# i and f rows inside the stick-breaking heads, two gates moved to the last head, transposes at the loop's front and values at its end

## The chip, the cores and the metric

The kernel runs on one core of one Trainium2 chip. The metric is the device time of one execution in microseconds (us). The profiled execution is taken apart below: PE is the matrix engine (TensorE), DVE the vector engine, ACT the scalar engine, POOL GpSimd, and SP the queue that issues most transfers. Each engine works through its own instructions in the order in which they were written to it; that order is fixed when the kernel is built.

## The reference, cut to what matters

One block of a hybrid encoder, 512 tokens of width 1024: stick-breaking attention (8 heads of 128), an mLSTM (4 heads of 256) and cross-attention (4 heads) read one normalised input; each branch is projected, gated and summed, then comes an MLP. The change concerns the first two branches, the gates and the first projections.

```python
def _stick_breaking(q, k, v):
    ...
        z = jnp.einsum('bhqd,bhkd->bhqk', qb, kf[:, :, :end]) * scale
        log_1m = jnp.where(causal, jax.nn.log_sigmoid(-z), 0.0)
        later = lax.cumsum(log_1m, axis=3, reverse=True) - log_1m
        log_a = jnp.where(causal, jax.nn.log_sigmoid(z) + later, -jnp.inf)
        outs.append(jnp.einsum('bhqk,bhkd->bhqd', jnp.exp(log_a), vf[:, :, :end]))
...
def _mlstm(q, k, v, i_pre, f_pre):
    log_f = jax.nn.log_sigmoid(f_pre.astype(f32))
    ...
        bcum = jnp.cumsum(lfc, axis=-1)
        d = jnp.where(tri, bcum[..., :, None] - bcum[..., None, :] + ic[..., None, :], -jnp.inf)
        m_t = jnp.maximum(m_inter, jnp.max(d, axis=-1))
...
        i_pre = (ml_i + b_if[l, :ML_HEADS]).transpose(0, 2, 1)
        f_pre = (ml_f + b_if[l, ML_HEADS:]).transpose(0, 2, 1)
...
        gates = jax.nn.sigmoid(gate_pre + b_gate[l]).reshape(bsz, seq, N_BRANCH, D_MODEL)
        mixed = (gates[:, :, 0] * (y_sb @ w_sb_proj[l])
                 + gates[:, :, 1] * (y_ml @ w_ml_proj[l])
                 + gates[:, :, 2] * (y_x @ w_x_proj[l]))
        x = x + mixed @ w_out[l]
```

## The kernel before, in words

Everything is kept in 128-partition tiles. A matrix product in near-f32 precision is made of three matmuls in a reduced format (`mm3`, L86 to L88): high by high, high by low, low by high. So a weight tile of 128x1024 (`load_w`, L80) is loaded by SP into one of 3 `raw` buffers, rounded by ACT into `whi` (L76), and its rest put by DVE into `wlo` (L77), 4 buffers of each. `projT` then runs 24 matmuls of 512 columns on it into one of two PSUM banks called `pj`. The banks called `tr` are two as well, those called `q4` four.

The stages in the order of time are the memory's keys and values, the products with V, O and gate weights, cross-attention, stick-breaking (about 350 to 512 us of the profile), then the projection of the stick-breaking result (`proj(0, ...)`), the mLSTM (to about 760 us), `proj(1, ...)`, the output product and the MLP.

The stick-breaking stage is a loop over 8 heads. Its parts are:

- `sb_qk(head)`: two `projT` (48 matmuls, in rows `pj<-h`) and the splits of q and k, for a head two ahead.
- `sb_weights(head)`: the scores z (10 matmuls into four `q4` banks, in rows `q<-k,q`), then per bank on DVE a mask (L764), on ACT Abs, Exp, Ln (L770 to L772), on DVE a minimum (L774) and a scan (L776), on ACT an Exp (L778) that gives A. The bank of 128 columns comes last.
- `sb_transposed(head)`: ten transposes of A (L789) into three `tr` tiles, for j=0 (4), j=1 (3) and j=2, 3 (3). The first transpose needs all four A tiles. As there are two `tr` banks, the third tile waits until the first has been split into `aT` by ACT and DVE (L93, L94).
- `sb_values(head)`: 10 matmuls (rows `tr<-aT,v`) into a `tr` bank, copied by ACT into `yf` (L812).
- `x_proj(n)`: n tiles of the cross-attention's projection (24 matmuls each, rows `pj<-y`); DVE multiplies each by its gate (L604, `mix<-pj,gate`).
- `y_pair`, `gate`: the split of a result into the input of `proj`; a sigmoid of 4 ACT and one DVE instruction (L130 to L134). `gate(0, ...)` and `gate(2, ...)` read finished sums from memory (`gd`), `gate(1, ...)` first runs a `projT`.

In the kernel before, the loop issues q and k, the x_proj tiles, the values of the head before, the scores of the next head, and the transposes of this head; the values of head 7 follow after the loop. Then come the i and f rows of the mLSTM: 16 matmuls (`tr<-h,wif`, L865, L866), a chain of ACT and DVE instructions on 4 partitions (L868 to L883) with two scans, the store of the result to memory, from where it is read back spread over all partitions, and 8 transposes of 4 columns (L898, L899) into the columns `acol` and `em`. Only the mLSTM needs them. In its heads 0, 1 and 2 stand the plain gates 0 to 2, 3 and 4.

A scheduler reorders what the code issues within each engine, by its own costs, so that the written order is a wish; the rows of the order below are what each engine gets.

Of the kernel before, what the change touches and what calls it, by code (L numbers as in the profile page):

```python
# [8 lines left out]
F32 = mybir.dt.float32  # L9
# [6 lines left out]
P = 128  # L16
# [19 lines left out]
def tile_block(ctx: ExitStack, tc: tile.TileContext, xT, x_, memT, mem_, small,  # L36
# [701 lines left out]
    def sb_qk(head):  # L738
        qp = tp.tile([P, 2, T], F32R, tag="qk", bufs=4, name="q")
        kp = tp.tile([P, 2, T], F32R, tag="qk", bufs=4, name="k")  # L740
        for isk, (t, scale) in enumerate(((qp, P ** -0.5), (kp, None))):
            if head < 2:
                o = raws[head, isk]
            else:
                o = pj()
                projT(h, load_w(w_sbqk[isk * NK + head]), o)
            split2(t, o, scale)
        q0 = tp.tile([P, P], F32, tag="q0", bufs=2, name="q0")
        k0 = tp.tile([P, P], F32, tag="k0", bufs=2, name="k0")
        whole(q0, qp[:, :, :P])  # L750
        whole(k0, kp[:, :, :P])
        qks[head] = qp, kp, q0, k0
# [71 lines left out]
    def y_pair(k):  # L824
        t = ytile()
        split2(t, y[k])
        return t

    x_proj.f = 0
    sb_qk(0)  # L830
    sb_weights(0)
    sb_v(0)
    sb_qk(1)
    aT = None
    for head in range(NK):
        if head < NK - 2:
            sb_qk(head + 2)
        x_proj((0, 1, 1, 1, 1, 2, 2, 0)[head])
        if head > 0:
            sb_values(head - 1, aT)  # L840
        if head == NK - 1:
            ys = [y_pair(k) for k in range(NK - 1)]
            gs = [gate(0, f) for f in range(3)]
        if head < NK - 1:
            if head % 2 == 0 and head < NK - 2:
                sb_v(head // 2 + 1)
            sb_weights(head + 1)
        aT = sb_transposed(head)
    sb_values(NK - 1, aT)
    y = ys + [y_pair(NK - 1)]  # L850
    ph.close()


    ph = ExitStack()
    tp = ph.enter_context(tc.tile_pool(name="mlp", bufs=1))


    raw = wp.tile([P, W], F32, tag="raw", bufs=3, name="raw")[:, :NK * NG].rearrange("p (k c) -> p k c", k=NK)
    wif = wp.tile([P, W], F32R, tag="whi", bufs=4, name="wif")[:, :NK * NG].rearrange("p (k c) -> p k c", k=NK)
    nc.sync.dma_start(out=raw, in_=w_if)  # L860
    act.activation(out=wif, in_=raw, func=AF.Copy)
    dve.tensor_tensor(out=wif[:, :, 64:], in0=raw[:, :, 64:], in1=f32(wif[:, :, 64:]), op=ALU.subtract)
    o = tr()
    for k in range(NK):
        pe.matmul(o[:NG, :], wif[:, k], h[k][:, 0, :], start=k == 0, stop=False)  # L865
        pe.matmul(o[:NG, :], wif[:, k], h[k][:, 1, :], start=False, stop=k == NK - 1)  # L866
    ip, fp, fa, mf, fc = (tmp(n)[:4, :] for n in ("ip", "fp", "fa", "mf", "fc"))
    act.activation(out=ip, in_=o[64:68, :], func=AF.Identity, bias=sm[0:4, C_BIF:C_BIF + 1])  # L868
    act.activation(out=fp, in_=o[96:100, :], func=AF.Identity, bias=sm[32:36, C_BIF:C_BIF + 1])
    dve.tensor_tensor(out=ip, in0=o[0:4, :], in1=ip, op=ALU.add)  # L870
    dve.tensor_tensor(out=fp, in0=o[32:36, :], in1=fp, op=ALU.add)
    act.activation(out=fa, in_=fp, func=AF.Abs)
    dve.tensor_scalar(out=mf, in0=fp, scalar1=0.0, scalar2=None, op0=ALU.min)
    act.activation(out=fa, in_=fa, func=AF.Exp, scale=-1.0)
    act.activation(out=fa, in_=fa, func=AF.Ln, bias=1.0)

    dve.tensor_tensor_scan(out=fc, data0=mf, data1=fa, initial=0.0, op0=ALU.add, op1=ALU.subtract)
    dve.tensor_tensor(out=ip, in0=ip, in1=fc, op=ALU.subtract)
    mr = tmp("mr")[:4, :]
    dve.tensor_tensor_scan(out=mr, data0=ip, data1=ip, initial=0.0, op0=ALU.max, op1=ALU.max)  # L880
    dve.tensor_tensor(out=fc, in0=fc, in1=mr, op=ALU.add)
    nm_ = tp.tile([4, T], F32, tag="nm", name="nm")
    dve.tensor_scalar(out=nm_, in0=mr, scalar1=-1.0, scalar2=None, op0=ALU.mult)  # L883

    nmd = dp.tile([4, T], F32, tag="nmd", name="nmd")
    nc.sync.dma_start(out=nmd, in_=nm_)

    def bcast(head):

        t = tp.tile([P, T], F32, tag="b1", bufs=2, name="b1")  # L890
# [2 lines left out]

    b1s = [bcast(0), bcast(1)]
    proj(0, y, gs)
    col = tr()
    for i in range(NT):
        pe.transpose(col[:, 4 * i:4 * i + 4], ip[:, i * P:(i + 1) * P], ident[:4, :4])  # L898
        pe.transpose(col[:, 16 + 4 * i:20 + 4 * i], fc[:, i * P:(i + 1) * P], ident[:4, :4])  # L899
    dve.tensor_copy(out=acol, in_=col[:, :16])  # L900
    act.activation(out=em, in_=col[:, 16:32], func=AF.Exp, scale=-1.0)
    y = [None] * NK
    vs, sos, qks = {}, {}, {}

# [48 lines left out]
    ml_qk(0)  # L953
    ml_v(0)
    ml_o(0)
    gs = []
    for head in range(4):
        q, k = qks[head][:2], qks[head][2:]

        sts, scs, b1 = [], [], b1s[head]  # L960
        bm = tmp("bm")
        dve.tensor_tensor(out=bm.rearrange("p (j c) -> p j c", j=NT), in0=b1.rearrange("p (j c) -> p j c", j=NT),
                          in1=m4.unsqueeze(1).to_broadcast([P, NT, P]), op=ALU.add)
        for j in range(NT):
            c0, c = j * P, slice(j * P, (j + 1) * P)
            st = q4()
            for f in range(2):
                if j < NT - 1:
                    mm3(st[:, c0:], k[f][0][:, 0, c], k[f][0][:, 1, c], q[f][0][:, 0, c0:], q[f][0][:, 1, c0:],
                        f == 0, f == 1)  # L970
                else:
                    pe.matmul(st[:, c0:], k[f][1], q[f][1], start=f == 0, stop=f == 1)
            sts.append(st)
        if head > 0:
            ml_y(head - 1, yts)
        for j in range(NT):
            c0 = j * P
            w = tmp("w")
            ab = acol[:, 4 * j + head:4 * j + head + 1]
            act.activation(out=w[:, c0:c0 + P], in_=bm[:, c0:c0 + P], func=AF.Exp, bias=ab)  # L980
            if j < NT - 1:
                act.activation(out=w[:, c0 + P:], in_=b1[:, c0 + P:], func=AF.Exp, bias=ab)
            dve.scalar_tensor_tensor(out=w[:, c0:], in0=sts[j][:, c0:], scalar=HD ** -0.5, in1=w[:, c0:],
                                     op0=ALU.mult, op1=ALU.mult)
            sc = tp.tile([P, 2, T - c0], F32R, tag=f"sc{j}", name="sc")
            split2(sc, w[:, c0:])
            scs.append(sc)
        if head < 2:
            b1s.append(bcast(head + 2))
        if head < 3:  # L990
            ml_qk(head + 1)
        else:
            gs += [gate(1, 5), gate(1, 6)]
        v, so = vs[head], sos[head]
        nms = []
        dn = tp.tile([P, NT], F32, tag="dn", bufs=2, name="dn")
        ss = tp.tile([P, NT], F32, tag="ssh", bufs=2, name="ssh")
        for i in range(NT):
            nm = q4()
            nms.append(nm)  # L1000
            for j in range(i + 1):
                c = slice((i - j) * P, (i - j + 1) * P)
                mm3(nm[:, :HD + 2], scs[j][:, 0, c], scs[j][:, 1, c], v[j][:, 0, :], v[j][:, 1, :], j == 0, j == i)
            d1 = dn[:, i:i + 1]
            dve.tensor_scalar(out=d1, in0=nm[:, HD:HD + 1], scalar1=-1.0, scalar2=None, op0=ALU.mult)
            dve.scalar_tensor_tensor(out=d1, in0=nm[:, HD:HD + 1], scalar=em[:, 4 * i + head:4 * i + head + 1],
                                     in1=d1, op0=ALU.max, op1=ALU.max)
            dve.reciprocal(out=d1, in_=d1)
            junk = tmp("junk")
            act.activation(out=junk[:, :HD], in_=nm[:, :HD], func=AF.Square, scale=d1, accum_out=ss[:, i:i + 1])  # L1010
        rr = rsqrt_cols(tp, ss, NT, 1.0 / HD, "rh")
        dve.tensor_tensor(out=dn, in0=rr, in1=dn, op=ALU.mult)
        yts = [tmp("yt") for _ in range(2)]
        for i in range(NT):
            c = slice((i % 2) * HD, (i % 2 + 1) * HD)
            dve.scalar_tensor_tensor(out=yts[i // 2][:, c], in0=nms[i][:, :HD], scalar=dn[:, i:i + 1],
                                     in1=so[:, i], op0=ALU.mult, op1=ALU.mult)
        if head < 3:
            gs += [gate(1, f, tr() if f == 2 else None) for f in ((0, 1, 2), (3,), (4,))[head]]
            ml_o(head + 1)  # L1020
            ml_v(head + 1)
        else:
            gs.append(gate(1, 7))
        if head == 3:
            ml_y(head, yts)
# [472 lines left out]
```

## Time and profile before

| | before |
|---|---|
| median of 3 runs | 1135.73 us (1135.08 to 1137.24) |
| the profiled execution | 1135.93 us, of which span 1134.2 us |
| PE busy | 1110.0 us, 98% of the span |
| DVE, ACT, POOL busy | 862.8, 727.6, 129.3 us |
| mean granted TensorE clock | 0.994 |

The span is the time from the first to the last instruction; 1.7 us of the profiled time lie outside it. Busy time of PE counts matmuls as they overlap, so what is left are the moments in which no matmul is under way. "Idle before" in a row is time in which the engine had nothing to do, and the name behind the arrow is what it then waited for last.

### The profile page before, as it was taken

The numbers are of one execution on the slowest core, as the hardware profiler recorded it, in microseconds if no ns is written. First come the engines' busy times: TensorE is split into PE (matmuls) and PEld (weight loads), VectorE is DVE, ScalarE is ACT, GpSimd is POOL, SyncE is SP. The second block draws the span as 40 slices with busy tenths as digits, with TensorE's granted clock in tenths as the row PEclk, the third lists the DMA queues.
The fourth block names the chain that finished last, engine by engine and source line by source line (L and its number), as shares of the span: only waits on it lengthen the run. The fifth ranks groups of instructions, "written<-read, shape, count | busy, mean of one in ns | idle before, by whom it ended". The sixth has DMA issues, their size and how long they took to land.

```text
span 1134.2 us, 16470 instructions
## 1 busy us (share of the span) xinstructions
PE 1110.0 (98%) x6080; PEld 957.8 (84%) x6080; DVE 862.8 (76%) x1267; ACT 727.6 (64%) x1208; POOL 129.3 (11%) x229
## 2 busy tenths in 40 slices
PE   9999999999999999986999999999999999999998
PEld 6778889999987888865888888888888898998997
DVE  5889777778767766666578798768867679688698
ACT  6756654648657867785477787735766466475573
POOL 0112211321101100000000000001011101111110
PEclk9999999999999999997999999999999999999999
DMA  9978888874512332225432322467377878878774
GB/s 358 352 193 236 249 231 273 227 233 143 183 40 96 117 105 96 84 65 177 140 101 88 103 89 75 158 167 157 113 206 169 209 181 204 202 205 212 172 192 112
DMA packets 62680, 190.31 MB, mean 168 GB/s; under 512 B 6788, under 2 KB 13572, under 8 KB 62600
## 3 DMA queue, kind: packets, MB, share of 16 engines
q1 hardware_dynamic: 45880, 131.25, 34.1%
q0 software_dynamic: 16288, 57.68, 24.6%
q8 instruction: 48, 0.79, 0.3%
q10 hardware_dynamic: 432, 0.33, 0.1%
q14 instruction: 32, 0.26, 0.1%
HBM read 172.45 MB, written 16.79 MB: 167 GB/s over the span
## 4 chain that ended last, share of the span: by engine, by line
PE 82%; DVE 8%; ACT 6%; issue 2%; DMA 1%; ACTq 0%; DVEq 0%; POOL 0%; POOLq 0%
PE pj L87 8%; PE pj L86 8%; PE pj L88 8%; PE q L170 5%; PE q L168 5%; PE q L169 5%; PE q L195 4%; PE q L196 4%; PE q L197 4%; PE q L86 3%; PE q L87 3%; PE q L88 3%; PE pj L168 2%; PE pj L169 2%; PE pj L170 2%; PE pj L196 2%
## 5 line engine op out<-in xcount | busy, mean ns | idle before, releaser
L76 ACT ACTIVATE whi<-rq 128x1024 fp32r<-128x1024 f32 x112 | 118.1, 1057 | 111.2 <-PE q L170 26.7
L77 DVE TENSOR_TENSOR wlo<-rq,whi 128x1024 fp32r<-128x1024 f32 x112 | 136.5, 1221 | 57.5 <-ACT whi L76 57.5
L76 ACT ACTIVATE whi<-B 128x1024 fp32r<-128x1024 f32 x84 | 88.5, 1058 | 77.1 <-PE q L196 16.5
L77 DVE TENSOR_TENSOR wlo<-B,whi 128x1024 fp32r<-128x1024 f32 x84 | 102.5, 1222 | 43.4 <-ACT whi L76 43.2
L86 PE MATMUL pj<-h,whi 128*128 128x512 f32 x296 | 116.9, 395 | 0.3 <-ACT mqk L93 0.3
L87 PE MATMUL pj<-h,whi 128*128 128x512 f32 x296 | 116.1, 392 | 0.0
L88 PE MATMUL pj<-h,wlo 128*128 128x512 f32 x296 | 115.9, 391 | 0.0
L76 ACT ACTIVATE whi<-raw 128x1024 fp32r<-128x1024 f32 x72 | 76.0, 1057 | 60.5 <-PE pj L87 47.5
L77 DVE TENSOR_TENSOR wlo<-raw,whi 128x1024 fp32r<-128x1024 f32 x72 | 87.8, 1221 | 31.5 <-ACT whi L76 31.4
L170 PE MATMUL q<-whi,slo 128*128 128x512 f32 (+1 forms) x236 | 91.1, 386 | 0.3 <-DVE slo L94 0.3
L169 PE MATMUL q<-wlo,shi 128*128 128x512 f32 (+1 forms) x236 | 91.1, 386 | 0.1
L168 PE MATMUL q<-whi,shi 128*128 128x512 f32 (+1 forms) x236 | 91.0, 386 | 0.0
L86 PE MATMUL pj<-y,whi 128*128 128x512 f32 x192 | 75.8, 396 | 1.9 <-DVE gt L607 1.9
L87 PE MATMUL pj<-y,whi 128*128 128x512 f32 x192 | 75.5, 393 | 0.0
L88 PE MATMUL pj<-y,wlo 128*128 128x512 f32 x192 | 75.3, 392 | 0.0
L202 POOL DMA_DIRECT2D rq<-in_w_ff_dram x50 | 42.9, 892 | 283.0 <-DVE wlo L77 173.9
L86 PEld LDWEIGHTS pj<-h,whi 128*128 128x128 f32 x296 | 55.6, 188 | 11.8 <-ACT mqk L93 0.7
L88 PEld LDWEIGHTS pj<-h,wlo 128*128 128x128 f32 x296 | 55.6, 188 | 11.3
L87 PEld LDWEIGHTS pj<-h,whi 128*128 128x128 f32 x296 | 55.6, 188 | 10.6
L170 PEld LDWEIGHTS q<-whi,slo 128*128 128x128 f32 x236 | 44.3, 188 | 9.6 <-DVE slo L94 0.7
L169 PEld LDWEIGHTS q<-wlo,shi 128*128 128x128 f32 x236 | 44.3, 188 | 9.3 <-DVE wlo L77 0.5
L168 PEld LDWEIGHTS q<-whi,shi 128*128 128x128 f32 x236 | 44.3, 188 | 8.9
(440 smaller groups left out, 3234.0 us busy)
## 6 DMA issues: line engine op xcount, KB each, us to landing
rq<-in_w_ff_dram SPq DMA_DIRECT2D x56, 512.0 KB, 4.7
rq<-in_w_ff_dram POOLq DMA_DIRECT2D x50, 512.0 KB, 5.7
B<-in_w_vo_dram SPq DMA_DIRECT2D x48, 512.0 KB, 5.5
B<-in_w_vo_dram POOLq DMA_DIRECT2D x24, 512.0 KB, 7.2
raw<-in_w_proj_dram SPq DMA_DIRECT2D x24, 512.0 KB, 3.6
raw<-in_w_sbqk_dram SPq DMA_DIRECT2D x16, 512.0 KB, 3.6
raw<-in_w_mlqk_dram SPq DMA_DIRECT2D x16, 512.0 KB, 3.6
rawk<-in_w_kv_dram SPq DMA_DIRECT2D x14, 512.0 KB, 8.5
```

What stands on the lines that cost most here:

```text
L76: act.activation(out=hi[:, c], in_=raw[:, c], func=AF.Copy)
L77: dve.tensor_tensor(out=lo[:, c], in0=raw[:, c], in1=f32(hi[:, c]), op=ALU.subtract)
L86: pe.matmul(out, lh, rh, start=start, stop=False)
L87: pe.matmul(out, lh, rl, start=False, stop=False)
L88: pe.matmul(out, ll, rh, start=False, stop=stop)
L168: pe.matmul(banks[j][:, c], lh, w[0][:, cw], start=st, stop=False, **mm)
L169: pe.matmul(banks[j][:, c], lh, w[1][:, cw], start=False, stop=False, **mm)
L170: pe.matmul(banks[j][:, c], ll, w[0][:, cw], start=False, stop=sp_, **mm)
L195: pe.matmul(o, wh, uh, start=start and k == 0 and f % 2 == 0, stop=False, **mm)
L196: pe.matmul(o, wh, ul, start=False, stop=False, **mm)
L197: pe.matmul(o, wl, uh, start=False, stop=stop and k == 3, **mm)
L202: pool.dma_start(out=raws[v], in_=w[fh, 2 * kh + v], accum_op=ALU.add)
```

## The change

The i and f rows become a function, `if_rows`, issued in turn 2 of the stick-breaking loop, and the small transposes another, `if_columns`, issued in turn 4. The tiles of the chain are reused in place. In the loop, the transposes of a head are issued first, then q and k, V, the scores of the next head, the x_proj tiles, and the head's own values last. In the last turn two plain gates, `gate(1, 0)` and `gate(1, 1)`, are issued; in the mLSTM head 0 keeps gate 2 alone. No instruction of PE is added or removed.

```diff
+    def if_rows():
+        ...
+        nc.sync.dma_start(out=raw, in_=w_if)
+        ...
+        for k in range(NK):
+            pe.matmul(o[:NG, :], wif[:, k], h[k][:, 0, :], start=k == 0, stop=False)
+            pe.matmul(o[:NG, :], wif[:, k], h[k][:, 1, :], start=False, stop=k == NK - 1)
+        ...
+        dve.tensor_tensor_scan(out=fp, data0=fp, data1=fa, initial=0.0, op0=ALU.add, op1=ALU.subtract)
+        dve.tensor_tensor(out=ip, in0=ip, in1=fp, op=ALU.subtract)
+        dve.tensor_tensor_scan(out=fa, data0=ip, data1=ip, initial=0.0, op0=ALU.max, op1=ALU.max)
+        ...
+        nc.sync.dma_start(out=nmd, in_=fa)
+        return ip, fp
+
+    def if_columns(ip, fc):
+        col = tr()
+        for i in range(NT):
+            pe.transpose(col[:, 4 * i:4 * i + 4], ip[:, i * P:(i + 1) * P], ident[:4, :4])
+            pe.transpose(col[:, 16 + 4 * i:20 + 4 * i], fc[:, i * P:(i + 1) * P], ident[:4, :4])
+        dve.tensor_copy(out=acol, in_=col[:, :16])
+        act.activation(out=em, in_=col[:, 16:32], func=AF.Exp, scale=-1.0)
...
-    aT = None
     for head in range(NK):
+        aT = sb_transposed(head)
         if head < NK - 2:
             sb_qk(head + 2)
+        if head < NK - 1:
+            if head % 2 == 1:
+                sb_v(head // 2 + 1)
+            sb_weights(head + 1)
+        if head == 2:
+            rows_if = if_rows()
+        if head == 4:
+            if_columns(*rows_if)
         x_proj((0, 1, 1, 1, 1, 2, 2, 0)[head])
-        if head > 0:
-            sb_values(head - 1, aT)
         if head == NK - 1:
             ys = [y_pair(k) for k in range(NK - 1)]
+            g1 = [gate(1, f) for f in range(2)]
             gs = [gate(0, f) for f in range(3)]
-        if head < NK - 1:
-            if head % 2 == 0 and head < NK - 2:
-                sb_v(head // 2 + 1)
-            sb_weights(head + 1)
-        aT = sb_transposed(head)
-    sb_values(NK - 1, aT)
+        sb_values(head, aT)
...
-    gs = []
+    gs = g1
     for head in range(4):
...
-            gs += [gate(1, f, tr() if f == 2 else None) for f in ((0, 1, 2), (3,), (4,))[head]]
+            gs += [gate(1, f, tr() if f == 2 else None) for f in ((2,), (3,), (4,))[head]]
```

What stands where on the engines, first on PE in a middle turn of the loop, before: the scores of head 6, the first seven transposes of head 5 right behind them, and projections.

```order
L86 MATMUL q_4660<-k,q 128x512
L87 MATMUL q_4660<-k,q 128x512
L88 MATMUL q_4660<-k,q 128x512
L761 MATMUL q_4674<-k_4358,q_4357 128x128
L789 MATMUL tr<-ident,A 128x128 x7
L86 MATMUL pj<-h,whi 128x512
L87 MATMUL pj<-h,whi 128x512
L88 MATMUL pj<-h,wlo 128x512
```

The same place of the change: the last matmul of a head's values, nine projections, and the first seven transposes of the next head.

```order
L809 MATMUL tr<-aT,v_4428 128x128
L86 MATMUL pj<-h,whi 128x512
L87 MATMUL pj<-h,whi 128x512
L88 MATMUL pj<-h,wlo 128x512
L86 MATMUL pj<-h,whi 128x512
L87 MATMUL pj<-h,whi 128x512
L88 MATMUL pj<-h,wlo 128x512
L86 MATMUL pj<-h,whi 128x512
L87 MATMUL pj<-h,whi 128x512
L88 MATMUL pj<-h,wlo 128x512
L789 MATMUL tr<-ident,A 128x128 x7
L86 MATMUL pj<-h,whi 128x512
```

The transposes of a head moved from one whole turn behind that head's scores to a place behind one x_proj tile (24 matmuls), the values and up to ten projections. In turn 2 the first four stand right behind the values of head 1, with no projection between.

Second, on PE behind the last head, before: the end of the i and f matmuls, six matmuls of `proj(0)` and the first small transpose.

```order
L866 MATMUL tr<-h,wif 100x512
L86 MATMUL pj<-y,whi 128x512
L87 MATMUL pj<-y,whi 128x512
L88 MATMUL pj<-y,wlo 128x512
L86 MATMUL pj<-y,whi 128x512
L87 MATMUL pj<-y,whi 128x512
L88 MATMUL pj<-y,wlo 128x512
L898 MATMUL tr<-ident,ip 128x4
L86 MATMUL pj<-y,whi 128x512
```

In the change the small transposes stand behind the scores of head 5, about one turn and a half behind the i and f matmuls.

```order
L761 MATMUL q_4684<-k_4422,q_4421 128x128
L865 MATMUL tr<-ident,ip 128x4
L866 MATMUL tr<-ident,fp 128x4
L865 MATMUL tr<-ident,ip 128x4
L866 MATMUL tr<-ident,fp 128x4
L865 MATMUL tr<-ident,ip 128x4
L866 MATMUL tr<-ident,fp 128x4
L865 MATMUL tr<-ident,ip 128x4
L866 MATMUL tr<-ident,fp 128x4
L86 MATMUL pj<-y,whi 128x512
```

So between the i and f matmuls and their small transposes there were six matmuls, and now there are a whole turn's.

Third, on ACT at the last head, before: the gates' sigmoids (L130 to L134) stand between the splits of head 7's transposed weights, `aT_5183` to `aT_5200`.

```order
L131 ACTIVATE gate_5172<-gate_5172 128x512
L93 ACTIVATE aT_5183<-tr_5178 128x512
L134 ACTIVATE gate_5164<-gate_5164,sm_70 128x512
L132 ACTIVATE gate_5172<-gate_5172 128x512
L93 ACTIVATE aT_5190<-tr_5186 128x384
L93 ACTIVATE aT_5197<-tr_5193 128x256
L134 ACTIVATE gate_5172<-gate_5172,sm_70 128x512
L794 ACTIVATE aT_5200<-tr_5193 128x128
L812 ACTIVATE yf_5213<-tr_5202 128x512
L93 ACTIVATE y_5215<-yf_5213 128x512
```

In the change they stand between those splits, which come first, and the copy `yf_5338` of head 7's values with its split `y_5340`. The gate 5297 is the plain gate 1.

```order
L132 ACTIVATE gate_5297<-gate_5297 128x512
L132 ACTIVATE gate_5305<-gate_5305 128x512
L130 ACTIVATE gate_5313<-gd_5311,sm_70 128x512
L134 ACTIVATE gate_5297<-gate_5297,sm_70 128x512
L134 ACTIVATE gate_5305<-gate_5305,sm_70 128x512
L131 ACTIVATE gate_5313<-gate_5313 128x512
L130 ACTIVATE gate_5321<-gd_5319,sm_70 128x512
L132 ACTIVATE gate_5313<-gate_5313 128x512
L131 ACTIVATE gate_5321<-gate_5321 128x512
L812 ACTIVATE yf_5338<-tr_5327 128x512
L134 ACTIVATE gate_5313<-gate_5313,sm_70 128x512
L93 ACTIVATE y_5340<-yf_5338 128x512
```

On PE the two plain gates (48 matmuls) now stand between the last transposes of head 7 and its values; behind the values, `proj(0)` runs the seven other heads' parts of its tile 0 and six of tile 1 (39 matmuls) before it reads head 7.

## Rows read from the trace of the kernel before

**Rows 1.** The page's part 1: span, busy time and instructions of each engine.

```profile
span 1134.2 us, 16470 instructions
PE 1110.0 (98%) x6080; PEld 957.8 (84%) x6080; DVE 862.8 (76%) x1267; ACT 727.6 (64%) x1208; POOL 129.3 (11%) x229
```

**Rows 2.** Waits of PE, whole span: total us, times, longest.

```profile
PE tr L898 <- DVE ip L878: 7.4, 1, 7.4
PE tr L789 <- DVE aT L94: 5.4, 7, 2.8
...
PE q L86 <- DVE A L776: 0.7, 1, 0.7
...
PE q L86 <- DVE yt L1016: 0.5, 2, 0.2
```

**Rows 3.** Windows: us, busy (x) of PE, PEld, DVE, ACT, POOL, clock, DMA, GB/s.

```profile
354.00:504.80 150.80, 147.37 (x721) 122.41 (x719) 105.69 (x180) 115.64 (x251) 10.00 (x36) 1.00 0.31 99
504.80:531.20 26.40, 13.31 (x48) 10.03 (x47) 16.49 (x25) 15.04 (x27) 1.05 (x8) 0.74 0.44 140
```

**Rows 4.** PE in order of time behind the last head: start, us, what, idle before.

```profile
507.77 0.52 PE L789 MATMUL tr<-ident,A 128*128 128x128 f32 x3 [2.80 <-DVE aT L94]
509.34 0.50 PE L86 MATMUL tr<-aT,v 128*128 128x512 f32 x1 [1.05 <-DVE aT L94]
...
527.52 0.80 PE L86 MATMUL pj<-y,whi 128*128 128x512 f32 x1 [1.86 <-DVE gt L607]
```

**Rows 5.** Windows of PE alone: us, busy (x), granted clock, DMA share, GB/s.

```profile
510.14:513.96 3.82, 3.82 (x15) 0.55 0.12 30
527.52:531.20 3.68, 3.68 (x10) 0.56 0.41 117
```

**Rows 6.** PE in order of time, inside the loop.

```profile
465.15 0.39 PE L86 MATMUL pj<-y,whi 128*128 128x512 f32 x1
...
470.59 0.39 PE L86 MATMUL tr<-aT,v 128*128 128x512 f32 x1
...
472.31 0.36 PE L86 MATMUL q<-k,q 128*128 128x256 f32 x1
...
488.55 0.36 PE L86 MATMUL q<-k,q 128*128 128x256 f32 x1
...
490.42 0.93 PE L789 MATMUL tr<-ident,A 128*128 128x128 f32 x7
```

**Rows 7.** Waits of PE from 354 to 504.8 us, the loop without its end.

```profile
PE tr L789 <- DVE aT L94: 2.6, 6, 0.5
```

**Rows 8.** DVE in order of time, inside the loop.

```profile
465.35 0.69 DVE L604 TENSOR_TENSOR mix<-pj,gate 128x512 f32<-128x512 f32 x1 [2.75 <-PE pj L88]
...
486.88 1.23 DVE L77 TENSOR_TENSOR wlo<-raw,whi 128x1024 fp32r<-128x1024 f32 x1
...
495.32 1.22 DVE L776 TENSOR_TENSOR_SCAN A<-q,a 128x511 f32<-128x511 f32 x1
496.46 0.26 DVE L774 SCALAR_TENSOR_TENSOR a<-q,a 128x127 f32<-128x127 f32 x1
...
497.24 0.41 DVE L776 TENSOR_TENSOR_SCAN A<-q,a 128x127 f32<-128x127 f32 x1
```

**Rows 9.** ACT in order of time, inside the loop and at its end.

```profile
480.91 0.29 ACT L778 ACTIVATE A<-A 128x128 f32<-128x128 f32 x1
...
497.68 0.31 ACT L778 ACTIVATE A<-A 128x128 f32<-128x128 f32 x1 [0.41 <-DVE A L776]
...
506.80 0.72 ACT L134 ACTIVATE gate<-gate,sm 128x512 f32<-128x512 f32 x1
507.41 0.63 ACT L132 ACTIVATE gate<-gate 128x512 f32<-128x512 f32 x1
...
512.26 0.60 ACT L812 ACTIVATE yf<-tr 128x512 f32<-128x512 f32 x1 [2.33 <-PE tr L809]
512.89 0.63 ACT L93 ACTIVATE y<-yf 128x512 fp32r<-128x512 f32 x1
```

More of the change, by code (lines that the diff above doesn't have):

```diff
@@ L827, in y_pair @@
         return t
+    nmd = dp.tile([4, T], F32, tag="nmd", name="nmd")
+    def if_rows():
+        raw = wp.tile([P, W], F32, tag="raw", bufs=3, name="raw")[:, :NK * NG].rearrange("p (k c) -> p k c", k=NK)
+        wif = wp.tile([P, W], F32R, tag="whi", bufs=4, name="wif")[:, :NK * NG].rearrange("p (k c) -> p k c", k=NK)
+        nc.sync.dma_start(out=raw, in_=w_if)
+        act.activation(out=wif, in_=raw, func=AF.Copy)
+        dve.tensor_tensor(out=wif[:, :, 64:], in0=raw[:, :, 64:], in1=f32(wif[:, :, 64:]), op=ALU.subtract)
+        o = tr()
+        for k in range(NK):
+            pe.matmul(o[:NG, :], wif[:, k], h[k][:, 0, :], start=k == 0, stop=False)
+            pe.matmul(o[:NG, :], wif[:, k], h[k][:, 1, :], start=False, stop=k == NK - 1)
+        ip, fp = (tp.tile([4, T], F32, tag=n, name=n) for n in ("ip", "fp"))
+        fa = tmp("fa")[:4, :]
+        act.activation(out=ip, in_=o[64:68, :], func=AF.Identity, bias=sm[0:4, C_BIF:C_BIF + 1])
+        act.activation(out=fp, in_=o[96:100, :], func=AF.Identity, bias=sm[32:36, C_BIF:C_BIF + 1])
+        dve.tensor_tensor(out=ip, in0=o[0:4, :], in1=ip, op=ALU.add)
+        dve.tensor_tensor(out=fp, in0=o[32:36, :], in1=fp, op=ALU.add)
+        act.activation(out=fa, in_=fp, func=AF.Abs)
+        dve.tensor_scalar(out=fp, in0=fp, scalar1=0.0, scalar2=None, op0=ALU.min)
+        act.activation(out=fa, in_=fa, func=AF.Exp, scale=-1.0)
+        act.activation(out=fa, in_=fa, func=AF.Ln, bias=1.0)
+        dve.tensor_tensor_scan(out=fp, data0=fp, data1=fa, initial=0.0, op0=ALU.add, op1=ALU.subtract)
+        dve.tensor_tensor(out=ip, in0=ip, in1=fp, op=ALU.subtract)
+        dve.tensor_tensor_scan(out=fa, data0=ip, data1=ip, initial=0.0, op0=ALU.max, op1=ALU.max)
+        dve.tensor_tensor(out=fp, in0=fp, in1=fa, op=ALU.add)
+        dve.tensor_scalar(out=fa, in0=fa, scalar1=-1.0, scalar2=None, op0=ALU.mult)
+        nc.sync.dma_start(out=nmd, in_=fa)
[7 more added lines that the diff above has]
+        act.activation(out=em, in_=col[:, 16:32], func=AF.Exp, scale=-1.0)
     x_proj.f = 0
@@ L855, in tile_block @@
     tp = ph.enter_context(tc.tile_pool(name="mlp", bufs=1))
[L858 to L886, printed above, removed]
     def bcast(head):
@@ L895, in tile_block @@
     proj(0, y, gs)
[L896 to L901, printed above, removed]
     y = [None] * NK
```

## The prediction, made before the change was run

> **What bounds the kernel now.** I read the page's first part first: PE is busy for 1110.0 of 1134.2 us [rows 1]. The change moves PE instructions and adds none, so it can win only from the 24.2 us in which PE has nothing under way, and from stretches in which its clock is low. The list of PE's waits says where those lie: one wait of 7.4 us of the first small transpose for the i and f chain (L898 on DVE's `ip`), and seven waits of the third transpose group (L789) of 5.4 us in all, of which one is 2.8 [rows 2]. Then the windows: from 354 to 504.8 us, the loop over the heads without its end, PE is busy for 147.4 of 150.8 us at clock 1.00; the next 26.4 us, to 531.2, hold only 13.3 us of PE work, at clock 0.74 [rows 3]. So one place holds more than half of what PE lacks. In order of time it reads so: the last three transposes of head 7 wait 2.80 us, its values 1.05, the small transpose 7.4, the next matmul of `proj(0)` 1.86 [rows 2, 4]. The order of ACT shows what stands behind the first two: the splits that free the `tr` bank stand behind three gates' sigmoids. The third waits for the whole chain from the i and f matmuls through ACT and DVE, with weight splits queued between on DVE; the fourth for a DVE instruction that stood behind the same chain.
>
> **What is removed.** The four waits: 2.80 + 1.05 + 7.4 + 1.86 = 13.1 us. Where they go: the chain now has a whole turn of the loop, over 70 matmuls, where it had six; the splits of head 7 stand ahead of the gates; and 48 matmuls of the plain gates lie between its transposes and its values. 24 matmuls of 512 columns take from 465.15 to 470.59, 5.44 us, or 0.227 each [rows 6], so the gates give 10.9 us of cover at the place where 3.85 were lost.
>
> **The clock.** Two stretches behind the waits ran at a granted clock of 0.55 and 0.56, near the lower of the two levels (1.2 of 2.4 GHz), for 3.82 and 3.68 us [rows 5]. Elsewhere in the loop it is 1.00 [rows 3]. If the waits go, so does this. By the clock alone it is worth 3.82 x 0.45 + 3.68 x 0.44 = 3.3 us; by the count of the second stretch, ten matmuls that would take 2.27 us at 0.227, it is 1.4 there against 1.6 by the clock. I take 3.0, bounds 2.8 and 3.3.
>
> **What the loop pays: the front transposes.** Before, a head's transposes came a turn after its scores and never waited for A. Now they come behind one x_proj tile, the values (470.59 to 472.31, 1.72 us) and 0 to 10 projections. Two chains decide. (a) From the first score matmul to the last A: 472.31 to 481.20, 8.9 us [rows 6, 9], which had a few splits and one gate step between. The cover from the same point is the scores themselves (488.55 to 490.42, 1.87), x_proj 5.44 and the values 1.72, together 9.0 without a projection, 11.3 with ten. (b) In heads 4 and 5 the DVE order puts x_proj's product with the gate (L604) ahead of the last scans. From the end of the x_proj tile on: start of L604 0.20 later (465.15 to 465.35), L604 0.69, the scan of 511 columns 1.22, 0.26, a weight split 1.23, the scan of 127 columns 0.41 and the Exp 0.31 [rows 6, 8, 9], 4.3 us; neighbours on one engine overlap by about 0.1, so 3.9 to 4.3. The cover is 1.72 plus nine or ten projections, 3.8 to 4.0. So the front transposes wait between 0 and 0.5 us a head. Head 3 has the 16 i and f matmuls as further cover, heads 6 and 7 have two x_proj tiles; that leaves heads 1, 2, 4 and 5, and head 0, whose values come right behind its transposes. Five times 0.3 is 1.5; bounds 0 and 5 (five times 1.0, if a transfer or a split is late as well). The six waits of the third group, 2.6 us [rows 7], have the same cause as before, one bank too few, and I leave them as they are; that they all go is the lower bound. The wait of 0.7 for a scan's bank at the loop's start [rows 2] isn't touched.
>
> **The i and f work inside the loop.** Its instructions on ACT and DVE are the same ones, queued in turn 2. Two of them stand on ACT ahead of head 3's last two Exps, which have the 16 i and f matmuls (3.6 us at 0.227) as cover that no other head has; the rest stand behind head 3's scans and ahead of the splits of its transposes, which are wanted only 19 projections later (4.3 us). I cost it at nothing, since ACT and DVE were busy for 116 and 106 of 150.8 us in the loop [rows 3]; without that slack it would be a wait of the length of the longest third-group wait inside the loop, 0.5 [rows 7]. The weight load of 400 KB and the small store move up in SP's queue, each with one `raw` buffer's turn ahead of it, and nobody waits for the store before the mLSTM.
>
> **The loop's end.** Head 7's values end the gates. ACT then has 13 gate steps before the copy `yf`, at 0.61 from start to start (506.80 to 507.41) 7.9 us, then 0.60, two more steps and the split, 0.63 [rows 9]: some 10.4 us from the end of the gates' matmuls. PE has the values, 1.72, and 39 matmuls that don't need it, 8.9 [rows 6]: 10.6. The gate tile that frees a `pj` bank for the third tile of `proj(0)` comes at about the same time. I take 0.3 us of wait, bounds 0 and 2 (as much as the present 1.86).
>
> **The mLSTM** loses 48 matmuls of cover behind its head 0; the order fills the place with projections of the next head. Heads with one gate behind them wait 0.2 us each now [rows 2]. I take 0.5 in all, bounds 0 and 2.
>
> **The sum.** 13.1 + 3.0 - 1.5 - 0.3 - 0.5 = 13.8 us off the profiled execution's 1135.93, of which 1134.2 is the span; that execution is 0.2 above the median of the runs. So 1122.1, said as **1122.0**.
>
> **A rule against it.** Before, single waits of up to 0.7 us inside the loop left the clock at 1.00 [rows 2, 3]; it fell only behind the long waits at the end [rows 4, 5]. The Trainium skill (TensorE: Matmul & The Clock Gate, section "A second HAM failure mode: psum-queue depth-cycling") says that short idles of PE between groups of matmuls, repeated each turn, can make the clock swing between its two levels, with a loss at each fall. By that rule the front waits that this change spreads over the loop would cost more than their own length; the trace so far disagrees with it.
>
> **The rivals.**
> 1. *The short front waits drop the clock.* Each of five would cost what a fall costs now, about 1.5 us [rows 5]: 7.5 more, 1129.5. Against it: clock 1.00 over the whole loop with seven waits in it. Chance 0.05. This is the mechanism of the rule above.
> 2. *The waits move into the loop, and the kernel is slower.* It needs the projections between values and transposes to be missing or late, so that the chains are met bare: 4.3 - 1.72 = 2.6 us in each of five heads, 13, and a fall of the clock behind each as behind the 2.80 of now, 7.5: 20.5 against 16.1, so 1140. It decides from 3.2 us a head on, clock included. Against it: the order has nine or ten projections there in two of the heads, and DVE and ACT have slack. Chance 0.03; a milder form, 2.5 to 3.2 a head, would end as no change, chance 0.04.
> 3. *Half of it:* front waits, head 7's split and the mLSTM reach their upper bounds (5 + 2 + 2), 1129, or some of them do, from 1125 on. Chance 0.15.
> 4. *Better than said:* the loop's waits vanish with the new order, 2.6 + 2.3 more, about 1117.2. Chance 0.10.
>
> **How the numbers follow.** The forecast's own case, 1119 to 1125, has 0.63. The range for 8 in 10 takes rival 4 in from 1117.5 and the larger part of rival 3, to 1128.0. A measurement of this kernel can tell about 0.2% (2.3 us) from no change. Faster by more: the forecast and rivals 1, 3 and 4, 0.93; within: 0.04; slower: 0.03.
>
> **What would show it.** In the changed profile the waits of the small transposes and of L607 should be gone from PE's list, and the window from the last head into `proj(0)` should be at clock 1.00. The loop should show a few waits of L789 for ACT's A (L778 or its line then) below 0.5 each. Wrong would be: a wait above 2 us anywhere in the loop, a granted clock below 0.95 in a window of the loop, or a wait of `proj(0)` for head 7's split. If PE's idle time fell by 13 us and the time didn't follow, the clock would have taken it.

## The result, and the profile after

The changed kernel takes 1123.09 us (median of 4 runs, 1122.05 to 1124.76) beside 1136.44 for the one before (4 runs, 1135.08 to 1137.24): a ratio of 0.9885, with a 95% interval from 0.9867 to 0.9903. The profiled execution took 1122.05 us, of which the span is 1120.3. Forecast were 1122.0 and 1120.4. The total was right; two of its terms were mis-sized in opposite directions, and what was said of why the waits go turned out to be wrong in part. Of the runs of the kernel before that are compared below, one took 3918.4 us and is left out of the ratios. The page's part 1 of the changed kernel, which answers to [rows 1]:

```profile
span 1120.3 us, 16473 instructions
...
PE 1106.8 (99%) x6080; PEld 954.9 (85%) x6080; DVE 859.7 (77%) x1267; ACT 728.2 (65%) x1208; POOL 126.6 (11%) x229
```

The waits of PE over the whole span, in the columns of [rows 2]:

```profile
PE q L86 <- ACT whi L76: 2.1, 2, 1.2
PE tr L789 <- ACT yf L812: 1.8, 3, 0.9
PE q L86 <- DVE yt L1021: 1.5, 2, 0.9
...
PE tr L789 <- DVE aT L94: 0.7, 1, 0.7
PE pj L86 <- DVE u L937: 0.6, 1, 0.6
PE tr L789 <- ACT A L778: 0.3, 1, 0.3
```

The 7.4, the 1.9 and the 2.8 are gone, and so is the values' 1.05. The loop's waits are about as long as before (2.6 and 2.8), but of another cause: three now wait for the copy `yf` of a head's values (L812), since values and transposes, which share the two `tr` banks, now stand close together; a single one, 0.3, waits for A. One more, 0.7 for the splits `aT`, is that of head 3. The mLSTM's waits (`yt`, `u`) have grown from 0.8 (with one for `mqk`, 0.3) to 2.1. The first row lies in the first 10 us, where these waits differ from run to run.

The windows that answer to [rows 3], in its columns: the loop as before, and behind it a stretch without a gap, at clock 1.00 where it was 0.74.

```profile
354.00:504.80 150.80, 147.20 (x722) 120.65 (x721) 111.17 (x192) 117.62 (x253) 7.81 (x36) 1.00 0.31 103
504.80:531.20 26.40, 26.40 (x119) 21.61 (x118) 14.61 (x21) 23.20 (x38) 1.10 (x8) 1.00 0.54 167
```

To see where the time came from, I cut each trace at three events that every version has: PE's first score matmul behind the wait at the loop's start (359.12 before, 358.37 after; from 357.1 to 359.1 in all the runs below, without an order in it), the first score matmul of the mLSTM, and the first transpose behind the mLSTM. Windows of PE alone: us, busy (matmuls), granted clock, DMA share, GB/s. Before:

```profile
359.12:591.34 232.22, 216.43 (x1015) 0.97 0.35 111
591.34:807.07 215.73, 214.91 (x1039) 1.00 0.42 120
359.12:1134.20 775.08, 754.73 (x3979) 0.99 0.54 144
```

After:

```profile
358.37:585.86 227.49, 224.62 (x1062) 1.00 0.37 118
585.86:793.16 207.30, 204.97 (x991) 1.00 0.42 120
358.37:1120.30 761.93, 752.99 (x3979) 1.00 0.54 147
```

From the loop's start to the end the change takes 775.08 - 761.93 = 13.15 us off; the rest of the span's 13.9 lies ahead of the loop, where nothing was changed. The two gates' 48 matmuls stand in the first window after and in the second before; at 0.227 each they are 10.9 us [rows 6]. Without them the first window went from 232.2 to 216.6, 15.6 less (forecast 13.1 + 3.0 - 1.5 - 0.3 = 14.3), and with them the mLSTM's went from 215.7 to 218.2, 2.5 more (forecast 0.5, bounds 0 and 2).

### The profile page after: what moved, and what is told of

It is laid out like the page before. It is cut to its first block, busy times and chain, and to the rows that moved or that the text cites. A ratio compares the mean times of both kernels' runs of the same rounds, so it can differ in the third digit from the quotient of the medians.

```text
span 1120.3 us, 16473 instructions
## 1 busy us (share of the span) xinstructions
PE 1106.8 (99%) x6080; PEld 954.9 (85%) x6080; DVE 859.7 (77%) x1267; ACT 728.2 (65%) x1208; POOL 126.6 (11%) x229
## 4 chain that ended last, share of the span: by engine, by line
PE 88%; ACT 5%; DVE 4%; issue 1%; DMA 1%; ACTq 0%; DVEq 0%
PE pj L86 8%; PE pj L87 8%; PE pj L88 8%; PE q L169 5%; PE q L170 5%; PE q L168 5%; PE q L195 4%; PE q L197 4%; PE q L196 4%; PE q L86 3%; PE q L88 3%; PE q L87 3%; PE pj L169 3%; PE pj L168 3%; PE pj L170 3%; PE pj L196 2%
```

## The experiments

Twelve kernels, in three groups, each beside runs of the kernel before on its chip (medians 1136.7, 1136.5, 1136.7). The two columns on the right are the two stretches just defined; the gates' 10.9 are taken off the first and put to the second where the gates stand in the last head.

| | edit | median us (range) | ratio, 95% | loop and proj(0) | mLSTM |
|---|---|---|---|---|---|
| | before | 1136.4 | 1 | 232.2 | 215.7 |
| | change | 1123.1 (1122.1-1124.8) | 0.9867-0.9903 | 216.6 | 218.2 |
| 1 | all undone, tiles of the change | 1130.4 (1129.8-1131.4) | 0.9932-0.9965 | 226.8 | 215.9 |
| 2 | i and f rows alone | 1126.3 (1125.4-1128.8) | 0.9898-0.9928 | 222.6 | 215.9 |
| 3 | gates alone | 1127.5 (1126.6-1128.9) | 0.9907-0.9936 | 222.6 | 218.2 |
| 4 | loop's order alone | 1119.0 (1118.2-1119.4) | 0.9830-0.9860 | 215.7 | 215.8 |
| 5 | loop's order on the kernel before | 1122.9 (1121.4-1124.2) | 0.9864-0.9897 | 220.3 | 215.7 |
| 6 | change without gates | 1120.3 (1118.9-1120.9) | 0.9840-0.9869 | 216.5 | 215.8 |
| 7 | change without i and f rows | 1121.3 (1120.9-1122.5) | 0.9852-0.9881 | 215.7 | 218.2 |
| 8 | change, scores late | 1120.8 (1120.2-1121.2) | 0.9845-0.9874 | 214.5 | 218.2 |
| 9 | before, one line moved | 1129.7 (1128.5-1130.8) | 0.9925-0.9958 | 226.6 | 215.7 |
| 10 | change without loop's order | 1122.5 (1121.9-1123.1) | 0.9862-0.9895 | 217.2 | 218.2 |
| 11 | 6 and 8 together | 1120.0 (1118.7-1120.2) | 0.9839-0.9869 | 216.1 | 215.8 |
| 12 | change again | 1122.9 (1121.5-1123.4) | 0.9865-0.9895 | 216.6 | 218.2 |

**1. All undone, but with the tiles of the change.** The order of `before`, with `if_rows()` and `if_columns()` called behind the loop; what is left of the change is that the chain writes over its own tiles:

```diff
-    ip, fp, fa, mf, fc = (tmp(n)[:4, :] for n in ("ip", "fp", "fa", "mf", "fc"))
+    ip, fp = (tp.tile([4, T], F32, tag=n, name=n) for n in ("ip", "fp"))
+    fa = tmp("fa")[:4, :]
```

> All three parts of the change are undone: i and f rows behind the loop, no gates of the second kind in the last head, a head's transposes and values in the old places. Only the tiles of the i and f chain are those of the change (each step writes over an earlier one's tile), and by the order this moves one thing: the kernel before had one small transpose ahead of 144 matmuls of proj(0), this kernel has all eight behind 150 of them. Theory of the prediction (the 7.4 us wait is there because the chain has no cover behind the loop): the chain stays where it was, so the wait stays in some form, 1136 us, at the least 1134. Rival (the wait came from the one early transpose, which held up 144 matmuls that didn't need it): the 7.4 goes, and with it 1.9 of the next wait and 1.4 of low clock, 10.7 in all: 1126 us, without a single move of the change. Bare wait alone: 1129.

1130.4, between the two values, 1136 and 1126. PE's waits show why:

```profile
PE tr L789 <- DVE aT L94: 5.3, 7, 2.8
PE pj L86 <- DVE gt L607: 4.1, 1, 4.1
...
PE tr L86 <- DVE aT L94: 1.1, 1, 1.1
```

The wait of 7.4 is gone without a move: it came from one small transpose that stood in PE's order ahead of 144 matmuls that didn't need it. But the wait for L607 grew from 1.86 to 4.06, so 5.2 of the 9.2 went. The rest is a matter of the chain's neighbours on DVE: the first two tiles of `proj(0)` end together, six matmuls behind the i and f matmuls, and the L607 that frees a bank for the third stands on DVE behind the chain's first steps and a weight split.

**2. The i and f rows alone**, in turns 2 and 4, and **3. the gates alone**:

```diff
+        if head == 2:
+            rows_if = if_rows()
+        if head == 4:
+            if_columns(*rows_if)
```

> Only the i and f rows and their columns are moved into the loop. Theory of the prediction: 7.4 + 1.9 of waits and 1.4 of clock go, the 2.8 + 1.05 of head 7's transposes and values stay with 1.6 of clock. New is that proj(0)'s first six matmuls of head 7's row no longer have the 16 i and f matmuls (3.6 us) ahead of them and wait about 2 for its split: 1136.4 - 10.7 + 2 = 1128 us. Rival (one early transpose): the same time as the kernel with all undone, within 2 us. Rival (work of i and f in the loop costs the loop): waits of more than 0.5 at head 3 in the loop, 1130 or more.

```diff
+            g1 = [gate(1, f) for f in range(2)]
             gs = [gate(0, f) for f in range(3)]
```

> Only the two plain gates are moved into the last head; i and f rows behind the loop, transposes and values in the old places. Theory of the prediction: the 48 matmuls cover head 7's transposes, so 2.8 + 1.05 of waits and 1.6 of clock go and the mLSTM pays 1.3: 1136.4 - 5.5 + 1.3 = 1132 us, with the wait of 7.4 in its place. Rival (one early transpose, which isn't there in this kernel either): 10.7 less than that, 1122 us, the time of the whole change.

With the rows alone 1126.3: the 7.4 and the 4.06 are gone, head 7's 2.80 and 1.05 stay, and as expected PE meets head 7's split behind its values:

```profile
515.00:517.00 2.00, 0.65 (x4) 0.84 0.11 42
516.85:518.00 1.15, 1.15 (x4) 1.00 0.65 203
```

This wait is 1.35 long (two windows of PE around its end), and the clock behind it is 1.00. The third theory's sign, a wait above 0.5 in the loop, is there too (0.69, for the chain's `fp` on DVE), but the loop's waits in all fell, from 2.6 to 2.0. With the gates alone, in PE's waits:

```profile
PE pj L86 <- DVE gt L607: 4.2, 1, 4.2
...
PE tr L86 <- DVE aT L94: 0.4, 1, 0.4
```

Head 7's 2.80 and 1.05 shrink to 0.35, so 48 matmuls of cover do remove them; the mLSTM pays, and the wait for L607 is there as in 1. The time, 1127.5, lies midway between the two expected, 1132 and 1122, since neither theory reckoned with the 4.2 for L607; that of 2 lies 1.7 us below the prediction's theory and 4.1 below kernel 1. Counted from kernel 1, each of the two edits takes 4.2 us out of 226.8.

**4. The loop's order alone.** The new loop without its four lines of `if_rows` and `if_columns` and without `g1`; the chain behind the loop, five gates in the mLSTM.

> Only the loop's order is changed: a head's transposes at the front, its values at the end; i and f rows behind the loop, all five gates of the second kind in the mLSTM. By the order the last head's values stand right behind its transposes. Theory of the prediction: the loop itself pays 0.2 as in the changed kernel, head 7's waits stay or grow (2.8 + 1.05 and up to 2 more), the 7.4 stays: 1136 to 1139 us. Rival (one early transpose): 10.7 less, 1126 to 1128 us.

1119.0: outside what either theory allowed, and 4 us faster than the whole change. Its stretches, in the columns of the windows above:

```profile
358.92:574.64 215.72, 213.40 (x1015) 1.00 0.36 119
574.64:790.46 215.82, 214.95 (x1038) 1.00 0.41 120
```

Neither head 7's waits nor that for L607 are in its list, though there are no gates and the chain hasn't moved. Two things were to be explained, and 5 and 9 were made for them. Its transposes' waits in the loop differ from the change's as well: four for A, in heads 2 to 5, and one for `yf`.

```profile
PE tr L789 <- ACT A L778: 1.8, 4, 0.6
...
PE tr L789 <- ACT yf L812: 0.4, 1, 0.4
```

**9. One line moved in the kernel before**: in the last turn `sb_transposed` stands ahead of the y splits and the three gates; all else is the kernel before.

```diff
         if head == NK - 1:
+            aT = sb_transposed(head)
             ys = [y_pair(k) for k in range(NK - 1)]
             gs = [gate(0, f) for f in range(3)]
         ...
-        aT = sb_transposed(head)
+            aT = sb_transposed(head)
```

The last line of the cut keeps the other turns as they were: it stands under `if head < NK - 1`.

> The kernel before with one line moved: in the last turn of the loop the transposes of head 7 are written ahead of the y splits and the three gates, not behind them. No gates moved, no i and f rows moved, the other turns as before. Theory that has come out of the runs so far (head 7's waits are there because the splits that free its banks stand on ACT behind three gates' sigmoids; it is ACT's order, not missing PE cover): the 2.8 and the 1.05 shrink to 0.5 or less together and give 1.6 of clock back; by the order 13 matmuls of proj(0), in place of six, stand behind the i and f matmuls, so the early small transpose waits 7.4 - 1.6 = 5.8; in sum 1136.5 - 3.4 - 1.6 - 1.6 = 1130 us. Theory of the prediction (48 matmuls of cover are needed): the two waits stay above 2.5 together, 1135 us or more.

1129.7. Head 7's two waits are gone altogether, with no matmul of cover added. ACT in order of time shows it. Before, the splits `aT` stand between the gates' steps:

```profile
505.80 0.62 ACT L131 ACTIVATE gate<-gate 128x512 f32<-128x512 f32 x1
506.32 0.58 ACT L93 ACTIVATE aT<-tr 128x512 fp32r<-128x512 f32 x1
...
507.93 0.78 ACT L93 ACTIVATE aT<-tr 128x384 fp32r<-128x384 f32 x2
508.85 0.72 ACT L134 ACTIVATE gate<-gate,sm 128x512 f32<-128x512 f32 x1
```

With the line moved the first two stand ahead of them, 5.5 to 6.2 us earlier when counted from the loop's start, though the seven transposes that they split run at the same time in both kernels (from 140.9 us on). Kernel 4 has them there too, by the loop's order. ACT of kernel 9:

```profile
499.04 0.60 ACT L93 ACTIVATE aT<-tr 128x512 fp32r<-128x512 f32 x1
499.53 0.62 ACT L93 ACTIVATE y<-yf 128x512 fp32r<-128x512 f32 x1
500.05 0.48 ACT L93 ACTIVATE aT<-tr 128x384 fp32r<-128x384 f32 x1
500.42 0.72 ACT L130 ACTIVATE gate<-gd,sm 128x512 f32<-128x512 f32 x1
```

On PE only four matmuls now stand between these seven transposes and the last three, where before there were 15 and a wait of 2.80. So the short, urgent splits waited on ACT for the longer steps issued ahead of them; it wasn't PE that lacked work to fill the gap. The expected 5.8 for the small transpose was wrong: it waits 7.1. On ACT the last steps of the gates now stand ahead of the chain, so that its `fp` starts 2.49 us behind the start of the last i and f matmul (509.55 and 507.06), before 1.14 (517.39 and 516.25); from there to the transpose it is 8.03 in both. The rows behind the transpose also price the clock: nine matmuls from 519.68 to 523.68 take 4.00 us where nine at 0.227 take 2.04.

```profile
510.40:517.58 7.18, 0.05 (x1) 0.72 0.43 123
...
519.68:522.00 2.32, 2.32 (x6) 0.50 0.19 73
522.00:524.00 2.00, 2.00 (x7) 0.54 0.48 123
524.00:526.00 2.00, 2.00 (x10) 1.00 0.90 286
```

**5. The loop's order on the kernel before**, with its tiles, so that the early transpose is back:

> The kernel before with the loop's new order and nothing else: the i and f chain with its own tiles, so one small transpose stands ahead of 144 matmuls of proj(0) again; but by the order 38 matmuls of proj(0) stand between the i and f matmuls and it, where the kernel before had six. Theory that has come out of the first four runs (what stands between the i and f matmuls and the early transpose is the cover; the loop's order gives it back, since the last head's transposes no longer use up these matmuls): 38 matmuls of 0.227 are 8.6 us, and the chain took 9.9 us from the last i and f matmul (503.9) to the end of ip (513.8) in the run with the loop's order alone, so the transpose waits 1.3 us, and the time is 1119 + 1.3 to 1119 + 2.8 with a fall of the clock: 1120.3 to 1121.8. Rival (the early transpose costs its 7.4 wherever the loop's order stands): 1126.5. Theory of the prediction: 1136 or more.

1122.9, and in PE's waits:

```profile
PE pj L86 <- DVE gt L607: 1.9, 1, 1.9
...
PE tr L895 <- DVE ip L875: 0.6, 1, 0.6
```

The transpose's 7.4 is down to 0.6 with 38 matmuls ahead of it, so the direction is as expected; a wait of 1.9 for L607 right behind it wasn't expected, and is more than the miss of 1.1 us (beyond 1121.8). So the loop's order brings the chain its cover too: head 7's transposes no longer use up the matmuls of `proj(0)` as filler, and these stand behind the i and f matmuls. In 4, where no small transpose stands among them, 182 do, and DVE takes the first L607 at 509.65, ahead of the chain's two scans; in 5 it comes behind both, at 512.77.

**6 and 7. The change without the gates, and without the i and f rows.** 6 leaves `g1` out and gives head 0 of the mLSTM its gates (0, 1, 2) again; 7 calls the two functions behind the loop.

> The change with the two plain gates back in the mLSTM: i and f rows inside the loop, the loop's new order. Theory of the prediction (the gates' 48 matmuls are the cover of head 7's transposes and values): without them 2.8 + 1.05 of waits come back and some of the 1.6 of clock; the mLSTM gets its 1.3 back: 1126 us. Rival (the loop's order alone brings the splits ahead of the gates' sigmoids, the cover isn't needed): the waits stay away, the mLSTM gets its 1.3 back: 1119 to 1121 us, as with the loop's order alone.

> The change with the i and f rows back behind the loop: the gates in the last head, the loop's new order. By the order 192 matmuls of proj(0) stand between the i and f matmuls and the small transposes. Theory of the prediction (the chain needs a turn of the loop as cover): a wait of proj(0) for L607, 1.9 or more, comes back with 1.4 of clock: 1126 us or more. Rival (192 matmuls cover it, and L607 is not held up since proj(0) has none of its tiles ready early): 1121 us, that of the loop's order alone and the mLSTM's 1.3 on top.

1120.3 and 1121.3, as the rivals said. In 6 head 7 waits for nothing, and the mLSTM has its old waits: 0.5 for `yt` in place of 1.5, none for `u`. The stretch of the mLSTM is 2.4 us shorter, of which 1.3 are listed waits; the other 1.1 isn't taken apart. Some of it lies in starts that come late by too little for the list (in the change 0.49 and 0.45 from one start to the next, at 622.49 and 639.04, where 0.23 is usual). In 7 the stretch up to the mLSTM is 0.9 us shorter than in the change: that is what the i and f rows cost the loop. Where, ACT of the changed kernel shows, ahead of its longest wait in the loop (PE's transposes at 412.74, 0.89 for `yf`): the chain's steps and two weight splits stand ahead of the copy.

```profile
407.75 1.04 ACT L76 ACTIVATE whi<-raw 128x1024 fp32r<-128x1024 f32 x1
408.70 0.61 ACT L849 ACTIVATE fa<-fp 4x512 f32<-4x512 f32 x1
409.22 1.04 ACT L76 ACTIVATE whi<-raw 128x1024 fp32r<-128x1024 f32 x1
410.17 0.61 ACT L851 ACTIVATE fa<-fa 4x512 f32<-4x512 f32 x1
410.82 0.63 ACT L852 ACTIVATE fa<-fa 4x512 f32<-4x512 f32 x1
411.36 0.70 ACT L130 ACTIVATE gate<-gd,sm 128x512 f32<-128x512 f32 x1
412.08 0.60 ACT L812 ACTIVATE yf<-tr 128x512 f32<-128x512 f32 x1
```

**8. Scores late.** The change with x_proj ahead of the next head's scores:

```diff
+        x_proj((0, 1, 1, 1, 1, 2, 2, 0)[head])
         if head < NK - 1:
             ...
             sb_weights(head + 1)
         ...
-        x_proj((0, 1, 1, 1, 1, 2, 2, 0)[head])
```

> The change with one thing moved: x_proj of a turn stands ahead of the next head's scores, not behind them, so that between a head's scores and its transposes there are only the values and what the order fills in, 20 to 22 projections. Theory of the prediction (chain a: 8.9 us from the first score matmul to the last A, against the cover from there): scores 1.87, values 1.72 and 20 projections of 0.227 are 8.1, so a front wait of 0.8 a head in heads 1 to 6, some 4 us: 1127 us, at the least the 1123 of the change. Rival (the waits move into the loop, above 2.6 us a head with a fall of the clock behind each): 1140 us.

1120.8, faster than the change, where slower was expected by both. PE's waits in the loop:

```profile
PE tr L789 <- ACT A L778: 1.0, 4, 0.3
...
PE tr L789 <- ACT yf L812: 0.5, 1, 0.5
```

The front waits for A come, but at 0.2 to 0.35 a head, not 0.8: the 8.9 us of chain a were read from a turn in which ACT and DVE did other work between its steps; that this work is done sooner with the scores late is my reading, which no run takes apart. And 20 projections now stand between values and transposes, so `yf` is mostly out of the `tr` bank in time: 1.5 us of waits instead of 2.8.

**10. The i and f rows and the gates, without the loop's order.**

> The change without the loop's new order: i and f rows inside the loop, two gates in the last head, transposes and values in the old places. Theory of the prediction (these two edits remove the four waits, the loop's order only makes room): the loop has its old 2.6 of waits, the mLSTM its 2.1, the four waits are gone, but the first matmuls of proj(0) for head 7's row meet its split with less ahead of them, 1.4 to 1.7 of wait as in the run with the i and f rows alone: 1123 + 1.6 = 1124.6 us. Rival (the gates also hold up ACT ahead of the values' copy): the wait for head 7's row grows to 3 or more, 1127 us.

1122.5. The wait for head 7's split is there as expected (1.35, and 0.32 for L607), the rest is better than expected; it isn't to be told from the change. So the four waits are removed in two different ways, down to 0.7 us that are left here (0.35 of head 7's values, 0.32 for L607): by the rows and the gates, or by the loop's order with the reused tiles (kernel 4).

**11. A version that the runs pointed to**, the edits of 6 and 8 together, and **12. the change again** beside it.

> A version that the runs point to: the change with the two gates back in the mLSTM (worth 1.3 of waits there) and with x_proj ahead of the next head's scores (front waits of 1.5 instead of 2.8 in the loop). The two parts sum up by the ledger of waits: 13.5 - 1.3 - 1.3 = 10.9 of PE's idle time or less, a span of 1117 to 1118, 1119 us; beside the change at 1123 a gain of 0.3%. Rival (the mLSTM or the loop's end gives it back, a wait of proj(0) for head 7's split of 1 to 2): 1121 us.

> The changed kernel itself, to have its time beside the version above on one chip: 1122 to 1124 us, the same waits in the loop and in the mLSTM to 0.1 us each, clock 1.00; what differs from its first profile lies in the first 10 us.

1120.0, midway between the two values expected, and 1122.9. The two gains don't add up: PE's list for 11 has two new waits at the loop's end. By the order on PE, 33 of the 42 matmuls of `proj(0)`'s first two tiles that don't need head 7's split went as filler ahead of its last values, and nine are left behind them; in kernel 6, without such a wait, ten went and 32 are left.

```profile
PE pj L86 <- ACT y L93: 0.7, 1, 0.7
...
PE pj L86 <- DVE gt L607: 0.3, 1, 0.3
```

The best kernel that was run is 4, the loop's order with the reused tiles and nothing else: 1119.0 us, its slowest run 2.1 us below the fastest of the change's eight. No run puts the tiles of 1 and the moved line of 9 together on the kernel before, so how much of the 16.5 us that 4 takes off the first stretch these two would give alone stays open.

## Why the prediction was right, and where it wasn't

- **What is removed**: 13.1 us of waits, all gone, and all that PE lacked behind the loop. The size was right; the reasons were only partly so. "The chain now has a whole turn of the loop" isn't what it needed: kernel 7 has the chain at its old place, with 192 matmuls of `proj(0)` ahead of its transposes, and no wait. "48 matmuls of the plain gates lie between its transposes and its values" would do (kernel 3), but isn't needed: kernels 4, 6 and 9 have no such cover and no wait. The prediction did name the splits' place ahead of the gates' sigmoids, but as one cause beside the cover; kernel 9 shows that it is enough.
- **The small transpose.** That one of the eight stood early in PE's order was in the order of before, and the prediction took its wait for one of the chain alone. Kernel 1 shows that 5.4 us of the stretch hang on that place.
- **The clock**: 3.0 forecast. Of the 15.6 us of the first stretch 13.1 are waits, and 0.2 more are spent in the loop, so some 2.7 are left for it. Counted directly, the two slow stretches of before cost 1.6 and 1.4 (the last section has the first). It came as said: no stretch below 1.00 behind the loop.
- **The loop's front waits**: 1.5 forecast. The change has a single wait for A, 0.32, and its loop's waits in all rose by 0.2. That is not because the chains were priced too dear: kernels 4, 5 and 7, which have the loop's order and no i and f rows in the loop, have four such waits of 0.32 to 0.60, 1.8 in all. The prediction took the loop's parts as independent, and they aren't. It left the third group's 2.6 as they are; with the loop's order alone they are down to one of 0.4. And with the rows in the loop the order on PE changes: in heads 2 and 3 the first four transposes stand right behind the values, and the next three wait for `yf` instead of A, 0.49 and 0.89. So the size came out small by a mechanism that it didn't have.
- **The i and f work inside the loop**: costed at nothing, else 0.5; it costs 0.7 (kernel 6 beside 4) to 0.9 (the change beside 7). The slack on ACT and DVE was an average over the loop; at head 3 the chain's steps hold up `yf` and then the splits `aT`, for waits of 0.89 and 0.71.
- **The loop's end**: 0.3 forecast, no wait there; within its bounds.
- **The mLSTM**: 0.5 forecast, bounds 0 and 2; measured 2.5, outside the bounds. This is the term that was most wrong. The "0.2 each" of heads with one gate was taken for the price of a missing gate; but head 0 lost 48 of its 72 matmuls, and the waits, at 645.80 (`u`), 657.83 and 694.09 (`yt`), reach into the heads behind it, which kept their one gate. Why the waits behind those heads grew, from 0.24 to 0.89 and 0.64, no run takes apart.
- **The rivals**: the first, that short waits drop the clock, is shown wrong here: the loop has waits up to 0.89 and is at 1.00 throughout. The rule beside it, of the Trainium skill (TensorE: Matmul & The Clock Gate, section "A second HAM failure mode: psum-queue depth-cycling"), did not show either: no swing between the levels in a loop of 150 us with five such waits. Whether more of them would bring it, no run here tells. The second, that the waits move into the loop, falls with the change itself and with kernel 8, whose longest waits in the loop are 0.89 and 0.48. The third, half of it, did not come either. The fourth, "better than said", was within reach: kernel 4 is at 1119.0, but by leaving two of the three edits out.

Of the signs of being wrong that it named, none came: no wait above 2 us in the loop, no window of it below 0.95, no wait for head 7's split (kernels 2, 10 and 11 have that one).

That the total agrees so well is partly luck: 1.6 us forecast too much for the loop's waits and its end, and 2.0 too little for the mLSTM, nearly cancel. Nor does all of the span's 13.9 belong to the change: 0.75 lie ahead of the loop.

## What to carry to other kernels

When a busy engine waits, look first at the order of the engine that it waits for: a short split behind three gates' longer steps cost 5.6 us here and was mended by moving a line (kernel 9), and one small transpose ahead of 144 matmuls cost 5.4 and went with another choice of tiles (kernel 1); neither needed more cover. Edits that aim at the same waits don't add up (the loop's order with the reused tiles takes 16.5 us off the first stretch, the whole change 15.6); run each alone before keeping all, since one that is no longer needed still charges its price (here 2.4 us in the mLSTM and 0.7 to 0.9 in the loop). Matmuls that could fill a gap are a stock: of the 192 of `proj(0)`, 42 stood ahead of the i and f matmuls before and 10 in kernel 4, which left 150 and 182 behind them.

## What the runs showed of the hardware

- The granted clock behind a wait of PE: at 1.00 behind waits of 0.89 (the change) and of 1.35 us (kernels 2 and 10); at 0.50 to 0.60 for 3.5 us behind the 0.61 and 1.91 of kernel 5, which have one short transpose between them, and at 0.50 to 0.54 for 4.0 us behind the 7.13 and 1.86 of kernel 9. A longer wait did not make the slow stretch much longer. The first of the two slow stretches of before, behind 2.80 and 1.05, cost 1.6: from the first 384-column matmul of head 7's values to the fifth i and f matmul it takes 3.59 us (510.14 to 513.73), and in kernel 9 at 1.00 2.04 (502.51 to 504.55). The one of kernel 9 cost 2.0.
- The stretch up to the loop, which has the same instructions in all runs, varies by 2 us (357.1 to 359.1), most of it in the first 15 us (waits for `whi` from 0.5 to 2.3 us in all), which is more than some of the effects here. Cutting the traces at common events took that out: two runs of the change then agreed to 0.1 us (761.93 and 761.88 from the loop's start to the end).
